# Input tiles from ScalarE's queue, and the bias tables' three copies issued apart, in a hybrid attention trunk layer

## The chip, the cores and the metric

One core of one Trainium2 chip. The metric is the device time of one execution in microseconds, the median of the runs.

## The reference

One layer of a diffusion trunk on 128 context tokens and 512 sample tokens of width 1024, all in float32. For both groups:

```
sh1, sc1, gt1, sh2, sc2, gt2 = adaln(c, w_mod, b_mod)
h = modulate(rmsnorm(x, g_mix_pre), sh1, sc1)
qa, ka, va, qb, kb, vb = project(h, w_in)
oa = neighborhood_attn(qa, ka, va, cache_a_k, cache_a_v, rpb_a)   # context tokens: full attention
ob = window_attn(qb, kb, vb, cache_b_k, cache_b_v, sink_b)
x = x + gt1 * rmsnorm(merge_heads(oa, ob, g_a, g_b, w_out), g_mix_post)
h = modulate(rmsnorm(x, g_ffn_pre), sh2, sc2)
x = x + gt2 * rmsnorm(conv_ffn(h, w_up, conv_w, conv_b, w_down), g_ffn_post)
```

The neighbourhood attention adds a bias to its scores that is gathered from `rpb_a` (8 heads, 15 x 31 entries): `bias = rpb[:, drow, dcol]`.

## The kernel before

A float32 product is made of three matmuls over high and low parts, so each weight block is loaded, rounded by ScalarE to its high part and subtracted by GpSimd or VectorE to its low part. The program is written out by hand in the order in which each engine gets its instructions; nothing reorders them later.

**The head.** `load_xt` (L200) loads five tiles of 128 tokens, xs0 to xs3 of the sample tokens in two halves each (64 rows picked by a pattern) and the context tokens as tile 4. For each tile `x_norm` takes ScalarE's square with a row sum (`junk`), GpSimd's root (`rxr`) and VectorE's scaling, and `x_trans` has PE transpose it into `xnT`. The modulation needs eight column blocks of `w_mod`, wm0 to wm7, each of two transfers of 512 KB (`load_wm`, L229); PE turns one into shift and scale by 16 small matmuls (`ada_a`, tile `psada`) and two more (`ada_c`, tile `pscol`).

**The v projection** is the loop over k = 0 to 7: `hidden(k)` makes block k of the modulated tokens, `va_mm(t, k)` adds its product for five token tiles into five PSUM banks (`psv`). The v weights come in four blocks vw0 to vw3 (`load_vw`, L236), each good for two k; `vw_split` makes the high part `vwh` on ScalarE and the low part `vwl` on GpSimd. At the end of each step k the loop issues later loads, ahead of the step's successor. The q and k projections (`psg`) follow and take 1024 x 128 blocks from a stream (`Stream`, tile `wst`): the first block wst0 is loaded at k = 2, the second at k = 4.

**The bias tables** are made in three stages through DRAM. `load_scr` (L241) has VectorE scale the 8 rows of `rpb_a` into two padded copies `rpx` and copies each of them 16 times into `scr`, in one transfer from 8 partitions. `load_ftab` (L249) copies `scr`, read with a skewed pattern, to `ftab` (1920 pieces of 128 bytes per transfer). `load_traw` reads one head's table back. Each stage waits for the one before it.

**Queues.** All loads are issued by SyncE (SP), in program order; ScalarE issues a few output transfers. A transfer tells of its landing by one of eight semaphores (DMAHW0 to DMAHW7 in the order listings), which are taken in turn over both queues, so a transfer that takes a semaphore again is issued only when its last user has landed.

Of the kernel before, what the change touches and what calls it, by code (L numbers as in the profile page):

```python
# [26 lines left out]
def trunk_kernel(  # L27
# [8 lines left out]
    nc = tc.nc  # L36
    xp = x_prompt[0]
# [36 lines left out]
    def U(shape, name, dt=F32):  # L74
        return up_.tile(shape, dt, tag="u", name=name)
# [3 lines left out]
    def WS(shape, name, i=None, dt=F32):  # L79
        if i is None:  # L80
            i = wsn[0] = 1 - wsn[0]
        return ws_.tile(shape, dt, tag=f"ws{i}", name=name)
# [13 lines left out]
    def SM(shape, name):  # L96
        return sm_.tile(shape, F32, tag="sm", name=name)
# [9 lines left out]
    def act(out, in_, func=ACTF.Copy, **kw):  # L107
        return nc.scalar.activation(out=out, in_=in_, func=func, **kw)  # L108
# [4 lines left out]
    def ts(out, a, s1, s2, op0, op1=None, eng=None):  # L113
        e = eng or nc.vector
        if op1 is None:
            return e.tensor_scalar(out=out, in0=a, scalar1=s1, scalar2=None, op0=op0)
        return e.tensor_scalar(out=out, in0=a, scalar1=s1, scalar2=s2, op0=op0, op1=op1)  # L117
# [59 lines left out]
    xt = [xp_[t // 2][:, t % 2, :] for t in range(5)]  # L177
    xsj = xs.rearrange("(r j c) d -> j r c d", r=8, j=8, c=8)
# [16 lines left out]
    def load_rows(n):  # L195
        for _ in range(n):
            src, dst = rows.pop(0)
            nc.sync.dma_start(out=dst, in_=src)

    def load_xt(t):  # L200
        if t == 4:
            nc.sync.dma_start(out=xt[4], in_=xp)
        else:
            for jj in range(2):
                nc.sync.dma_start(out=xt[t][jj * 64:jj * 64 + 64, :], in_=xsj[2 * t + jj])

# [6 lines left out]
    def rev(ap, o, n):  # L215
        return bass.AP(tensor=ap.tensor, offset=ap.offset + 14 * 31 + o, ap=[list(ap.ap[0]), [-31, 15], [1, n]])
# [7 lines left out]
    def load_late():  # L224
        nc.sync.dma_start(out=rp, in_=rpb_a[0])
        nc.sync.dma_start(
            out=sink, in_=sink_b[0].rearrange("a b -> (a b)").unsqueeze(0).to_broadcast([128, 8]))

    def load_wm(k):  # L229

        t = wm[k] = U([128, 2, KD, 128], f"wm{k}")
        for i in range(2):
            o = i * D + k * 128
            nc.sync.dma_start(out=t[:, i], in_=wmod[:, o:o + 128].rearrange("(k p) f -> p k f", p=128))

    def load_vw(st):  # L236
        w = WS([128, 2, 512], "vw")
        nc.sync.dma_start(
            out=w, in_=win[st * 256:st * 256 + 256, 1024:1536].rearrange("(k p) f -> p k f", p=128))
        vw[st] = w  # L240

    def load_scr():
        ts(rpx[0][:, :, 15:31], rev(rp, 7, 16), 8.0, None, ALU.mult)
        ts(rpx[1][:, :, 8:39], rev(rp, 0, 31), 8.0, None, ALU.mult)
        for v in range(2):
            nc.sync.dma_start(
                out=scr[v].rearrange("q (h a) w -> h q (a w)", h=8),
                in_=rpx[v].rearrange("p a w -> p (a w)").unsqueeze(1).to_broadcast([8, 16, 720]),
            )  # L249

    def load_ftab():
        for v in range(2):
            sv = scr[v, 0]
            nc.sync.dma_start(
                out=ftab[v].rearrange("q (a k) -> q a k", k=32),
                in_=bass.AP(tensor=sv.tensor, offset=sv.offset + 15, ap=[[120 * PW - 1, 16], [PW, 120], [1, 32]]),
            )
# [3 lines left out]
    def load_traw(h):  # L261
        traw[h] = t = PB([128, 2, 256], f"traw{h}")
        for v in range(2):
            for jj in range(2):
                fv = ftab[v]
                nc.sync.dma_start(
                    out=t[jj * 64:jj * 64 + 64, v, :],
                    in_=bass.AP(tensor=fv.tensor, offset=fv.offset + jj * 8 * 3840 + h * 480,
                                ap=[[32, 8], [3840, 8], [1, 256]]))

    load_xt(0)
    load_xt(1)
    load_xt(2)
    load_rows(2)
    load_xt(3)
    load_wm(0)
    load_xt(4)
    load_rows(3)
    load_vw(0)
    load_wm(1)  # L280
    load_wm(2)
    load_vw(1)
    load_wm(3)
    load_late()
    load_rows(6)
    load_wm(4)
    load_wm(5)
# [44 lines left out]
    def rows_late():  # L332
        ps = PS("o", "psr1")
        nc.tensor.transpose(ps[:, 0:32], rows1[96:128, :], ident[96:128, 96:128])
        nc.vector.tensor_copy(T1[:, 72:104], ps[:, 0:32])
        for o, n in ((W_GF, 8), (W_GMP, 16)):
            ts(T1[:, o:o + n], T1[:, o:o + n], D ** 0.5, None, ALU.mult, eng=nc.gpsimd)
        ts(nsink, sink, -1.0, None, ALU.mult, eng=nc.gpsimd)
# [63 lines left out]
    def ada_a(k, i):  # L402
        if i == 0:
            mps[k] = PS("o", "psada")
        ada_mm(mps[k], lambda j: wm[k][:, i, j, :], 128 * i, 128)
        if i == 1:
            m = PB([128, 512], "m_sb")
            act(m[:, 0:256], mps[k][:, 0:256])
            mps[k] = m

    def ada_c(k):
        ps_ = PS("s", "pscol")
        m = mps[k]
        for i in range(2):
            nc.tensor.matmul(ps_[:, 2 * i:2 * i + 2], m[:, i * 128:i * 128 + 128], sel[:, 0:2], start=True, stop=True)
        bb = lambda i: T1[:, W_MODT + 8 * i + k:W_MODT + 8 * i + k + 1].to_broadcast([128, 2])
        tt(S1[:, k, :], ps_[:, 0:2], bb(0), ALU.add)
        tmp = SM([128, 2], "gtmp")
        tt(tmp, ps_[:, 2:4], bb(1), ALU.add)
        ts(G1[:, k, :], tmp, 1.0, T1[:, W_GM + k:W_GM + k + 1], ALU.add, ALU.mult)  # L420

    def vw_split(st):
        wh = wr_.tile([128, 2, 512], F32R, tag="wh", name="vwh")
        wl = wr_.tile([128, 2, 512], F32R, tag="wl", name="vwl")
        for j in (slice(0, 1), slice(1, 2)) if st == 0 else (slice(0, 2),):
            act(wh[:, j], vw[st][:, j])
            tt(wl[:, j], vw[st][:, j], f(wh[:, j]), ALU.subtract, eng=nc.gpsimd)
        vwt[st] = (wh, wl)

    def hidden(k):  # L430
        kb, kk = k // 4, k % 4
        if k == 4:
            hH[1] = U([128, 4, T], "hH1", F32R)
            hL[1] = U([128, 4, T], "hL1", F32R)
        hf = QT([128, T], "hf")
        for c_, t_ in ((slice(512, 640), 0), (slice(0, 512), 1)):
            g_, s_ = G1[:, k, t_:t_ + 1], S1[:, k, t_:t_ + 1]
            act(hH[kb][:, kk, c_], xnT[kb][:, kk, c_], ACTF.Identity, scale=g_, bias=s_)
            ts(hf[:, c_], xnT[kb][:, kk, c_], g_, s_, ALU.mult, ALU.add)
        tt(hL[kb][:, kk, :], hf, f(hH[kb][:, kk, :]), ALU.subtract)  # L440
        for hx, hs in ((hxH, hH[kb]), (hxL, hL[kb])):
            nc.gpsimd.tensor_copy(hx[:, k, 0:64], f(hs[:, kk, 448:512]))
            nc.gpsimd.tensor_copy(hx[:, k, 64:128], f(hs[:, kk, 0:64]))

    def va_mm(t, k):
        wh, wl = vwt[k // 2]
        l_ = (hxH[:, k, :], hxL[:, k, :]) if t == 1 else (hh(k, 0, VS[t]), hh(k, 1, VS[t]))
        mm3(pv_[t], l_[0], l_[1], wh[:, k % 2, :], wl[:, k % 2, :], k == 0, k == KD - 1)
# [3 lines left out]
    def load_cc(p):  # L452
        cc = CC[p] = FP([128, 3, 128], "cc")
        nc.sync.dma_start(out=cc[:, 0], in_=ck_a[:, p * 128:p * 128 + 128])
        nc.sync.dma_start(out=cc[:, 1], in_=cv_a[:, p * 128:p * 128 + 128])
# [15 lines left out]
    for k in range(KD - 1):  # L471
        for j, t in enumerate(VO):
            va_mm(t, k)
            if j == 1:
                ada_c(k + 1)
                hidden(k + 1)
                if k == 6:
                    stream.split()
            if j == 3 and k < 6:
                ada_a(k + 2, 0)  # L480
                ada_a(k + 2, 1)
        if k % 2 == 0 and k < 6:
            vw_split(k // 2 + 1)
        if k < 2:
            load_wm(k + 6)
        if k == 2:
            load_vw(3)
            stream.load()
            rows_late()
        if k == 3:  # L490
            act(SM([128, 1], "warm"), zero, ACTF.Exp)
        if k == 4:
            load_scr()
            load_ftab()
            stream.load()
            load_cc(0)
        if k == 5:
            load_traw(0)
            load_traw(1)
# [1494 lines left out]
```

## Time and profile before

| what | value |
|---|---|
| median of 3 runs | 863.63 us (859.67 to 864.28) |
| the profiled execution, its own time | 864.4 us |
| its span, first to last instruction | 862.6 us |
| PE matmuls busy | 804.0 us, 93% of the span |
| VectorE, ScalarE, GpSimd busy | 562.8, 435.5, 295.5 us |
| mean granted TensorE clock | 0.985 |
| moved by DMA | 107.77 MB, 125 GB/s over the span |

Times in rows are microseconds from the span's start. A busy PE is counted by modelled ends of pipelined matmuls. The idle time that a timeline shows in brackets is that of the engine just before the instruction, with what ended it.

### The profile page before, as it was taken

Reading aid. Unit: us, or ns where it says so; the run is one execution under the profiler, and the core shown is the slowest. Engines: PE = TensorE matmul, PEld = TensorE weight load, DVE = VectorE, ACT = ScalarE, POOL = GpSimd, SP = SyncE. Lnnn points to the kernel's source line nnn. Section 1 sums busy time; section 2 is a strip of 40 time slices with the busy share of each in tenths; the row PEclk is TensorE's granted clock in tenths of the full one; section 3 lists DMA queues with packets and bytes.
Section 4 is the critical chain, followed back from the end, with each engine's and each line's share of the span. In section 5 each row is a group of like instructions: output and inputs, shape, how many; then the busy total and the mean of one; then the engine's idle time right before and its main releaser. Section 6 shows DMA issues by size and latency. Waiting matters only on the chain.

```text
span 862.6 us, 13868 instructions
## 1 busy us (share of the span) xinstructions
PE 804.0 (93%) x5280; PEld 702.5 (81%) x5280; DVE 562.8 (65%) x1023; ACT 435.5 (50%) x876; POOL 295.5 (34%) x353
## 2 busy tenths in 40 slices
PE   2897999999999999998989999999999999999996
PEld 2666878888778777868988999999999988888885
DVE  1543566655788885476479898898898874332115
ACT  3443567745578886457346445455455544332112
POOL 1443244424131211155954564564564200000001
PEclk9899999999999998999999999999999999999999
DMA  6996644363522122657223333332432336534313
GB/s 140 267 241 112 177 140 129 111 171 101 130 74 75 25 74 68 205 182 211 73 65 100 109 113 93 116 113 82 126 115 80 123 105 222 173 113 154 118 49 122
DMA packets 144277, 107.77 MB, mean 125 GB/s; under 512 B 16440, under 2 KB 125268, under 8 KB 144212
## 3 DMA queue, kind: packets, MB, share of 16 engines
q1 hardware_dynamic: 143204, 106.25, 42.0%
q8 instruction: 41, 0.67, 0.3%
q10 hardware_dynamic: 1008, 0.66, 0.3%
q14 instruction: 24, 0.20, 0.1%
HBM read 93.02 MB, written 14.36 MB: 124 GB/s over the span
## 4 chain that ended last, share of the span: by engine, by line
PE 46%; DVE 29%; DMA 9%; ACT 8%; issue 5%; SPq 2%; POOL 1%; DVEq 0%; POOLq 0%; ACTq 0%
PE psd L127 18%; PE psg L127 9%; DVE cv L120 7%; DVE ou L111 4%; DVE cv L111 4%; DVE owl L111 3%; PE psya L127 3%; PE zx L127 3%; PE psS L127 2%; PE psyb L127 2%; ACT cv L108 2%; DVE yy L111 2%; DMA scr<-rpx 2%; PE psO L127 2%; ACT P L108 2%
## 5 line engine op out<-in xcount | busy, mean ns | idle before, releaser
L127 PE MATMUL psd<-dwh,a 128*128 128x512 f32 x440 | 138.4, 395 | 0.0
L111 POOL TENSOR_TENSOR wsum<-wraw 128x512 f32<-128x512 f32 x36 | 70.4, 1976 | 105.3 <-DVE osb L111 50.6
L127 PEld LDWEIGHTS psd<-dwh,a 128*128 128x128 f32 x440 | 83.0, 189 | 19.9 <-ACT dwh L108 0.2
L127 PE MATMUL zx<-h2H,ou 128*128 128x322 f32 x392 | 94.9, 312 | 1.4 <-DVE yy L111 0.9
L127 PE MATMUL psd<-dwl,a 128*128 128x512 f32 x220 | 87.2, 397 | 0.8 <-DVE dwl L111 0.8
L111 DVE TENSOR_TENSOR dwl<-wd,dwh 128x1024 fp32r<-128x1024 f32 x22 | 26.9, 1225 | 89.7 <-ACT dwh L108 89.7
L127 PE MATMUL psg<-hH,wh 128*128 128x320 f32 x224 | 76.4, 341 | 7.4 <-ACT T L108 3.4
L108 ACT ACTIVATE dwh<-wd 128x1024 fp32r<-128x1024 f32 x22 | 23.3, 1059 | 94.4 <-PE psd L127 87.5
L127 PE MATMUL psg<-hH,wl 128*128 128x320 f32 x224 | 70.5, 315 | 0.0
L127 PE MATMUL psg<-hL,wh 128*128 128x320 f32 x224 | 70.5, 315 | 0.0
L127 PEld LDWEIGHTS zx<-h2H,ou 128*128 128x128 f32 x392 | 68.0, 189 | 2.0 <-DVE yy L111 1.2
L117 POOL TENSOR_SCALAR rdv<-ssdc 128x1 f32<-128x1 f32 x5 | 1.5, 300 | 179.1 <-ACT jk L108 179.1
L127 PE MATMUL zx<-h2L,ou 128*128 128x322 f32 x196 | 60.8, 310 | 0.0
L127 PEld LDWEIGHTS psg<-hH,wh 128*128 128x128 f32 x224 | 43.1, 192 | 16.7 <-ACT T L108 7.2
L108 ACT ACTIVATE cv<-yy,T 128x642 f32<-128x642 f32 x20 | 17.7, 885 | 65.7 <-DVE yy L111 65.7
L127 PEld LDWEIGHTS psd<-dwl,a 128*128 128x128 f32 x220 | 41.4, 188 | 10.8 <-DVE dwl L111 1.1
L120 DVE SCALAR_TENSOR_TENSOR cv<-yy,T,cv 128x641 f32<-128x641 f32 x40 | 35.4, 884 | 17.9 <-ACT cv L108 17.2
L127 PE MATMUL yy<-tg,oc 128*128 128x322 f32 x216 | 39.1, 318 | 5.7 <-DVE oc L111 5.7
L111 POOL TENSOR_TENSOR wl<-wst,wh 128x1024 fp32r<-128x1024 f32 (+1 forms) x12 | 27.7, 2311 | 48.3 <-ACT wh L108 31.6
L127 PEld LDWEIGHTS psg<-hL,wh 128*128 128x128 f32 x224 | 43.2, 193 | 0.5
L127 PEld LDWEIGHTS psg<-hH,wl 128*128 128x128 f32 x224 | 43.0, 192 | 0.0
L108 ACT ACTIVATE P<-P,nm 128x320 f32<-128x320 f32 (+3 forms) x64 | 40.3, 630 | 3.7 <-DVE nm L639 3.4
(352 smaller groups left out, 2215.1 us busy)
## 6 DMA issues: line engine op xcount, KB each, us to landing
wraw<-in_w_up_dram SPq DMA_DIRECT2D x40, 512.0 KB
wms<-in_w_mod_dram SPq DMA_DIRECT2D x32, 512.0 KB
wd<-in_w_down_dram SPq DMA_DIRECT2D x22, 512.0 KB
wm<-in_w_mod_dram SPq DMA_DIRECT2D x16, 512.0 KB
aD<-cv SPq DMA_DIRECT2D x22, 321.0 KB
ar<-aD SPq DMA_DIRECT2D x11, 642.0 KB
wst<-in_w_in_dram SPq DMA_DIRECT2D x10, 512.0 KB
yD<-Y SPq DMA_DIRECT2D x5, 512.0 KB
```

The lines of the kernel that those rows point to most:

```text
L108: return nc.scalar.activation(out=out, in_=in_, func=func, **kw)
L111: return (eng or nc.vector).tensor_tensor(out=out, in0=a, in1=b, op=op)
L117: return e.tensor_scalar(out=out, in0=a, scalar1=s1, scalar2=s2, op0=op0, op1=op1)
L120: return nc.vector.scalar_tensor_tensor(out=out, in0=a, scalar=s, in1=b, op0=op0, op1=op1)
L127: return nc.tensor.matmul(out, l, r, start=start, stop=stop, skip_group_check=True, **kw)
```

## The change

Four things move. `load_xt` takes a queue: tile 0 stays on SP, tiles 1 to 4 are issued by ScalarE, ahead of its first square. On SP, the first v block stands ahead of `b_mod` and its companions, and `load_late` (the bias table's source and the sinks) stands two blocks earlier. `load_scr` is called at k = 0 instead of k = 4. `load_ftab` is called at k = 3; at k = 4 the second streamed block is now the first load.

```diff
-    def load_xt(t):
+    def load_xt(t, eng):
         if t == 4:
-            nc.sync.dma_start(out=xt[4], in_=xp)
+            eng.dma_start(out=xt[4], in_=xp)
         else:
             for jj in range(2):
-                nc.sync.dma_start(out=xt[t][jj * 64:jj * 64 + 64, :], in_=xsj[2 * t + jj])
+                eng.dma_start(out=xt[t][jj * 64:jj * 64 + 64, :], in_=xsj[2 * t + jj])
...
-    load_xt(0)
-    load_xt(1)
-    load_xt(2)
+    load_xt(0, nc.sync)
+    load_xt(1, nc.scalar)
     load_rows(2)
-    load_xt(3)
+    load_xt(2, nc.scalar)
     load_wm(0)
-    load_xt(4)
+    load_xt(3, nc.scalar)
+    load_vw(0)
+    load_xt(4, nc.scalar)
     load_rows(3)
-    load_vw(0)
     load_wm(1)
+    load_late()
     load_wm(2)
     load_vw(1)
     load_wm(3)
-    load_late()
     load_rows(6)
...
         if k < 2:
             load_wm(k + 6)
+        if k == 0:
+            load_scr()
         if k == 2:
             load_vw(3)
             stream.load()
             rows_late()
         if k == 3:
             act(SM([128, 1], "warm"), zero, ACTF.Exp)
+        if k == 3:
+            load_ftab()
         if k == 4:
-            load_scr()
-            load_ftab()
             stream.load()
             load_cc(0)
```

ScalarE at the program's start, before (`junk,ssx` is the square of a tile; xs_128 holds tiles 0 and 1, xs_129 tiles 2 and 3, xs_130 tile 4):

```order
L108 ACTIVATE cpad<-cst 128x1 [waits DVE_49]
L108 ACTIVATE junk,ssx<-xs_128 128x1024 [waits DMAHW1_49,DMAHW0_49]
L108 ACTIVATE junk,ssx<-xs_128 128x1024 [waits DMAHW3_49,DMAHW2_49]
L108 ACTIVATE xnT_182<-pxs 128x4x128 [waits PE_49]
L108 ACTIVATE junk,ssx<-xs_129 128x1024 [waits DMAHW5_49,DMAHW4_49,Activation_49]
```

and now:

```order
L108 ACTIVATE cpad<-cst 128x1 [waits DVE_49]
L205 DMA xs_128<-in_x_sample_dram 64x1x1024 x2
L205 DMA xs_129<-in_x_sample_dram 64x1x1024
L205 DMA xs_129<-in_x_sample_dram 64x1x1024 [waits DMAHW0_49]
L205 DMA xs_129<-in_x_sample_dram 64x1x1024 [waits DMAHW2_49]
L205 DMA xs_129<-in_x_sample_dram 64x1x1024 [waits DMAHW4_49]
L202 DMA xs_130<-in_x_prompt_dram 128x1024 [waits DMAHW7_49]
L108 ACTIVATE junk,ssx<-xs_128 128x1024 [waits DMAHW3_49,DMAHW1_49]
```

Seven transfers now stand ahead of the first square. The four with a wait stand behind the landing of both halves of tile 1 (semaphores 0 and 2), of the first half of tile 2 (4), and of the transfer that took semaphore 7 first, SP's fifth one that has no wait, the first half of wm0.

SP in the v projection's loop, before (wm_416 is wm6, wm_470 wm7, the second `vw` vw3, the first `wst` wst0):

```order
L238 DMA vw<-in_w_in_dram 128x2x512 [waits DMAHW4_49,Pool_49]
L234 DMA wm_416<-in_w_mod_dram 128x8x128 [waits DMAHW5_49]
L234 DMA wm_416<-in_w_mod_dram 128x8x128 [waits DMAHW6_49]
L234 DMA wm_470<-in_w_mod_dram 128x8x128 [waits DMAHW7_49,PE_49]
L234 DMA wm_470<-in_w_mod_dram 128x8x128 [waits DMAHW0_49]
L238 DMA vw<-in_w_in_dram 128x2x512 [waits DMAHW1_49,Pool_49]
L350 DMA wst<-in_w_in_dram 128x8x128 [waits DMAHW4_49,DMAHW2_49,Pool_49]
L246 DMA scr<-rpx 8x16x720 [waits DMAHW3_49,DVE_49]
L246 DMA scr<-rpx 8x16x720 [waits DVE_49]
L254 DMA ftab<-scr 1920x1x32 [waits DMAHW5_49,DMAHW3_49]
L254 DMA ftab<-scr 1920x1x32 [waits DMAHW6_49,DMAHW4_49]
L350 DMA wst<-in_w_in_dram 128x8x128 [waits DMAHW7_49,DMAHW1_49,Pool_49]
```

and now:

```order
L238 DMA vw<-in_w_in_dram 128x2x512 [waits DMAHW4_49,Pool_49]
L234 DMA wm_416<-in_w_mod_dram 128x8x128 [waits DMAHW5_49]
L234 DMA wm_416<-in_w_mod_dram 128x8x128 [waits DMAHW6_49]
L246 DMA scr<-rpx 8x16x720 [waits DMAHW7_49,DVE_49]
L246 DMA scr<-rpx 8x16x720 [waits DMAHW0_49,DVE_49]
L234 DMA wm_474<-in_w_mod_dram 128x8x128 [waits DMAHW1_49,PE_49]
L234 DMA wm_474<-in_w_mod_dram 128x8x128 [waits DMAHW2_49]
L238 DMA vw<-in_w_in_dram 128x2x512 [waits DMAHW3_49,Pool_49]
L351 DMA wst<-in_w_in_dram 128x8x128 [waits DMAHW4_49,DMAHW2_49,Pool_49]
L254 DMA ftab<-scr 1920x1x32 [waits DMAHW7_49,DMAHW5_49]
L254 DMA ftab<-scr 1920x1x32 [waits DMAHW6_49,DMAHW0_49]
L351 DMA wst<-in_w_in_dram 128x8x128 [waits DMAHW3_49,Pool_49]
```

The two `scr` copies went from behind the first streamed block to a place right behind wm6 and ahead of wm7, vw3 and that block; `ftab` still stands behind it and ahead of the second block.

## Rows read from the trace of the kernel before

**Rows 1.** The page, busy time of PE (share of the span)

```profile
PE 804.0 (93%) x5280; PEld 702.5 (81%) x5280; DVE 562.8 (65%) x1023; ACT 435.5 (50%) x876; POOL 295.5 (34%) x353
```

**Rows 2.** The chain of waits, 0 to 140 us: start, length, what

```profile
3.51 9.96 DMA xs<-in_x_sample_dram
...
43.12 8.14 DMA vw<-in_w_in_dram
...
60.37 15.67 DMA scr<-rpx
76.06 0.56 SPq L254
76.72 5.95 DMA wst<-in_w_in_dram
```

**Rows 3.** Timeline of PE: start, length, what, idle before and what ended it

```profile
22.13 0.65 PE L383 MATMUL psada<-wm,cpad 128*32 128x128 f32 x16 [0.82 <-DMA wm<-in_w_mod_dram]
...
31.74 0.50 PE L127 MATMUL psv<-vwh,hH 128*128 128x512 f32 x1
...
54.91 0.51 PE L127 MATMUL psv<-vwl,hH 128*128 128x512 f32 x1 [1.23 <-POOL vwl L111]
...
65.73 0.39 PE L127 MATMUL psv<-vwl,hH 128*128 128x512 f32 x1
...
78.56 0.38 PE L127 MATMUL psg<-hH,wh 128*128 128x320 f32 x1 [1.67 <-DVE V L111]
...
83.77 0.33 PE L618 MATMUL pst<-ident,cc 128*128 128x128 f32 x1 [1.44 <-DMA cc<-in_cache_a_k_dram]
...
86.18 0.63 PE L127 MATMUL psg<-hH,wh 128*128 128x320 f32 x1 [2.09 <-DVE q L111]
```

**Rows 4.** Windows, PE: stretch, length, busy (x), granted clock, DMA share, GB/s

```profile
42.00:60.00 18.00, 16.60 (x156) 1.00 1.12 297
...
60.50:70.00 9.50, 9.50 (x73) 1.00 0.47 51
70.00:71.60 1.60, 1.60 (x8) 1.00 0.98 125
71.80:75.20 3.40, 3.40 (x21) 1.00 0.47 50
75.20:76.80 1.60, 1.60 (x12) 1.00 0.54 87
86.20:89.50 3.30, 3.30 (x12) 0.50 0.86 239
89.50:92.00 2.50, 2.50 (x18) 0.99 0.78 227
```

**Rows 5.** Timeline of SP's queue: start, length of issue, transfers

```profile
13.49 6.49 SPq L202 DMA_DIRECT2D xs<-in_x_prompt_dram  x1
...
46.02 6.86 SPq L234 DMA_DIRECT2D wm<-in_w_mod_dram  x4
52.98 1.68 SPq L238 DMA_DIRECT2D vw<-in_w_in_dram  x1
...
60.01 0.68 SPq L246 DMA_DIRECT2D scr<-rpx  x2
68.88 7.74 SPq L254 DMA_DIRECT2D ftab<-scr  x2
```

**Rows 6.** Timeline of ScalarE

```profile
7.49 1.06 ACT L108 ACTIVATE junk<-xs 128x1024 fp32r<-128x1024 f32 x1 [5.28 <-DMA xs<-in_x_sample_dram]
...
25.17 1.06 ACT L108 ACTIVATE junk<-xs 128x1024 fp32r<-128x1024 f32 x1 [2.85 <-DMA xs<-in_x_prompt_dram]
...
59.98 1.05 ACT L108 ACTIVATE vwh<-vw 128x1024 fp32r<-128x1024 f32 x1
...
72.72 4.20 ACTq L1167 DMA_DIRECT2D out_dram<-vo  x1
```

**Rows 7.** Timeline of GpSimd, the low half of vw3

```profile
61.12 2.39 POOL L111 TENSOR_TENSOR vwl<-vw,vwh 128x1024 fp32r<-128x1024 f32 x1 [0.54 <-ACT vwh L108]
```

## The prediction

> **What bounds the kernel now.** I read the page first, for the engine that fills the span: PE is busy for 93% of it [rows 1]. So time is lost or won only where PE waits, or where it runs at the lower clock. The change touches the first 95 us, and the next view is the chain of waits there. It shows what ended last: after the first input tiles, the third streamed weight block of the v projection (vw, issued at 43.12), then 15.67 us of the copy `scr<-rpx`, then the block `wst` issued only at 76.72 [rows 2]. The reader should see that the chain stands on transfers there, while PE was mostly busy beside them.
>
> The timeline of PE tells what that cost. The v projection's first matmul is at 31.74. PE idles 1.23 us at 54.91, and then 1.67, 1.44 and 2.09 us before 78.56, 83.77 and 86.18, together 5.20 us [rows 3]. After the last of these it restarts at the lower of its two clock levels: in the window from 86.2 to 89.5 the granted clock is 0.50 (1.2 GHz) and 12 matmuls take 3.3 us, while from 89.5 on 18 take 2.5 us [rows 4]. Twelve at that pace are 1.67 us, so the restart loses 1.6 us. These 6.8 us are all that the second half of the change can give back.
>
> The windows on the DMA engines come last, and they decide the case. From 42 to 60 us the engines are full (share 1.12, 297 GB/s): the weights arrive just in time. From 60.5 to 70, with only the two `scr` copies under way, the share is 0.47 at 51 GB/s: half of the engines are busy, slowly. At 68.88 SP issues the first `ftab` copy [rows 5]. The rate rises to 125 GB/s with a share of 0.98 until 71.6, falls back to 50 until 75.2, and rises again to 87 when the second `scr` copy ends [rows 4]. So the idle half of the engines did its part of `ftab` at once, and the other half did its part only after `scr`: an engine serves SP's transfers in the order of issue, and `scr` holds about eight of the sixteen.
>
> **Part by part.** *1. The `scr` copies move up, from behind all weights to a place ahead of wm7, vw3 and wst0.* They are issued at k = 0 now, and SP reaches them right after wm6. In the trace SP starts wm6 and wm7 (four transfers) at 46.02 and vw3 at 52.98 [rows 5]; VectorE's `rpx` now stands behind the second hidden block and is long done. What `scr` was behind before and is ahead of now is wm7 (2 x 0.52 MB), vw3 (0.52) and wst0 (0.52), 2.1 MB, at 297 GB/s 7.0 us. The copies began to move at about 60.4, after their issue at 60.01 [rows 5], so now at about 53.4. The second copy took 7.2 us after the first (SP's two `ftab` issues, each released by one of them, are at 68.88 and 76.06 [rows 2, 5]), so two need 14.4, and they hold half of the engines until 67.8. A weight transfer is spread over all engines and is not there until the blocked half has done its share, so wm7 and vw3 (1.57 MB, 5.3 us) land at about 73.1.
>
> Who waits: ScalarE's split of vw3 started at 59.98 without idling [rows 6], and GpSimd's half of that split ended at 61.12 + 2.39 = 63.51 [rows 7], 3.5 us after it. Now it ends at 73.1 + 3.5 = 76.6. PE's first matmul with its result ran at 65.73 [rows 3]. **Term: 76.6 - 65.7 = +10.9 us.** The bounds are the landing of vw3. If the earlier start of the weights at the head saves the pauses of the engines there, it is 2 us sooner; if `scr` moves more slowly beside the weights, as the full share of 1.12 allows, 3 us later: +8.9 to +13.9. I take 10.9, since in rows 4 `scr` kept its pace (51 and 50 GB/s) with and without waiting copies behind it. wm7 lands before vw3 and adds nothing.
>
> *2. `ftab` and the second streamed block.* In the trace both waited for `scr` to land (SP at 68.88 for 7.74 us [rows 5], `wst` at 76.72). Now `ftab` is issued once wst0 is, near 75, and the block once GpSimd has left its buffer, near 78; with the 5.95 us of rows 2 it is there at 84, and PE asks for it at 76.6 plus the 15 us of matmuls that lie between 65.73 and 86.18 (20.45 less the 5.20 idle), so at 92. The idle 1.44 and 2.09 us go. The 1.67 us come from ScalarE, held for 4.20 us in the issue of an output at 72.72 [rows 6] while `scr` and `ftab` filled the queue; that issue is now at about 84, behind both. **Term: -5.2 us.** Bounds: -5.2, and -3.5 if that hold stays.
>
> *3. Clock.* PE stands nearly idle for ten microseconds before 76.6, longer than before 86.18, so it will restart at 0.50. The 1.6 us move from one place to the other. **Term: 0**, between -1.6 (it doesn't fall) and +1.6 (it falls twice).
>
> *4. Input tiles on ScalarE's queue.* Transfers take eight completion semaphores in turn over both queues, and one that reuses a semaphore is issued when its last transfer has landed. ScalarE must issue all seven transfers before its first square, and the last (the prompt tile) waits for the first half of wm0. Before, the first square ran at 7.49, the last at 25.17, and PE started the v projection 6.6 us after that [rows 3, 6]. Now the first square runs at the earliest when xs2's first half has landed and the tile is issued (SP's wait for that half ended at 13.49 [rows 5], plus 1, so 14.5), at the latest when wm0 is there (PE's wait for it ended at 22.13 [rows 3]). Behind ScalarE's wait stand the five squares, and behind each GpSimd's root, VectorE's scaling and PE's transposes. All tiles have nearly arrived by then; with 1.06 us for a square and as much again for the copy and the hand-overs to the next one, I estimate 9 us from the first square to the last. The last is at 24 to 31, the v projection starts at 31 to 38. I take 35.5, +4, between -1 and +6. **Term: 0**, because PE would be that much later at 65.7 and then wait that much less for vw3; the cover is the 10.9 us of part 1. Without it the price is 4 less the 1.2 us idled at 54.91, since vw2 would no longer be late: +2.8.
>
> *5. vw0, the table's source rows and the rows of gains* change places by one or two transfers within the full stretch; 0, under the same cover.
>
> **Sum.** +10.9 - 5.2 + 0 + 0 = +5.7 us on the profiled execution of 864.4, so 870.1. That execution is 0.8 above the median of the runs shown, so I forecast 869.3 for the median. Over the bounds the sum runs from 8.9 - 5.2 - 1.6 = +2.1 to 13.9 - 3.5 + 1.6 = +12.0.
>
> **The rivals.** *Faster: the copies do not hold the weights.* If `scr` leaves its engines free for the weights behind it, vw3 lands by 62.2 and PE never waits: 5.2 and 1.6 us go, and the median is 856.8. For it: the copy moves only 51 GB/s, which leaves most of what the engines can carry. Against it: `ftab` stood still behind `scr` on just these engines [rows 4]. It decides at vw3: each microsecond after 62.2 costs one, and beyond 69 us nothing is left of the gain. The Trainium skill (DMA: Bandwidth & Descriptors, section Anatomy of one DMA) gives 2.0 us plus the bytes over 436 GB/s for a transfer; that would be an estimated 2.8 us for each 0.37 MB copy, vw3 at 64.4, and a median of 859.0. It is a fit for transfers of GpSimd, and the trace disagrees: 15.67 us for the two.
>
> *No change: copies harmless, head late.* Then part 4 loses its cover: -6.8 + 2.8 = -4.0, 859.6. For it stands the order in which ScalarE issues; against it the same rows as above. The Trainium skill (same page, section Issuing engines are not separate DMA queues) says that starting transfers on several engines saves only the time of the sequencer that starts them. By that the head would come out as before, 856.8 in this case. SP's prompt tile took 6.49 us to issue [rows 5], so here the sequencer's time is not small, and no run yet shows two queues loading at once.
>
> *Balance.* vw3 lands near 68 and what it costs is what the later stalls give: 863.6.
>
> *Slower still.* `scr` takes a third longer among the weights: 4.8 us more, 874.
>
> **How the numbers follow.** The forecast, with its bounds, gets 0.66; copies harmless 0.12; harmless with a late head 0.10; balance 0.05; slower still 0.07. A measurement of this kernel tells about 0.5%, 4.3 us, from no change: below 859.3 is faster, above 867.9 slower. Of the forecast's 0.66 I put 0.16 under 867.9, since its middle is only 1.4 above that. Faster is 0.12, no change 0.16 + 0.10 + 0.05 = 0.31, slower 0.50 + 0.07 = 0.57. The range 859.5 to 877 leaves out the 0.12 below and some 0.05 above. The forecast's own range, from its bounds, is 866 to 875.
>
> **What would show it.** Right: in the changed trace ScalarE's split of vw3 starts near 73 and PE idles some 10 us before the v projection's k = 6, split between wm7's side matmuls and vw3; the window after 54 us shows a DMA share near 0.5; PE has no wait between 78 and 95 but those of restart; the first square is at 14 to 22. Wrong: vw3 split before 63, or PE without a wait over 3 us there; or the first 140 us as long as before with the loss elsewhere, which would mean that work after the tables absorbed it.

## The result, and the profile after

The changed kernel takes 868.92 us (median of 13 runs, 866.2 to 873.95). The kernel before takes 863.63 in 13 runs beside it. The ratio of the two over these runs is 1.0058, with a 95% interval from 1.0036 to 1.0081: about 5 us slower. The profiled execution has a span of 866.7 us against 862.6, that is 4.1 more, with a mean granted clock of 0.983 against 0.985.

The page of the changed kernel, busy times [rows 1] and the queue that carries ScalarE's transfers (packets, MB, share of the engines; before, 1008 packets and 0.66 MB):

```profile
PE 803.4 (93%) x5280; PEld 703.0 (81%) x5280; DVE 562.2 (65%) x1023; ACT 435.8 (50%) x876; POOL 294.7 (34%) x353
...
q10 hardware_dynamic: 1584, 2.75, 1.3%
```

PE is busy for as long as before, so its busy time does not show the loss; its waits and its clock do. The chain of waits of the changed kernel, 0 to 140 us [rows 2] (start, length, what):

```profile
60.91 10.57 DMA vw<-in_w_in_dram
71.56 1.07 ACT vwh L108
72.70 2.35 POOL vwl L111
75.10 2.76 PE psv L127 x5
```

The copy `scr<-rpx`, 15.67 us long in the chain of before, has left it. In its place stands the last v block vw3, on its way for 10.57 us, and behind it one after the other ScalarE's rounding, GpSimd's low half and PE. SP's queue [rows 5] and the windows on PE [rows 4] (stretch, length, busy of PE, PEld, DVE, ACT and POOL with instructions, granted clock, DMA share, GB/s) tell why:

```profile
48.61 2.55 SPq L246 DMA_DIRECT2D scr<-rpx  x2
51.25 9.56 SPq L234 DMA_DIRECT2D wm<-in_w_mod_dram  x2
60.91 5.74 SPq L238 DMA_DIRECT2D vw<-in_w_in_dram  x1
66.74 0.42 SPq L351 DMA_DIRECT2D wst<-in_w_in_dram  x1
67.25 5.55 SPq L254 DMA_DIRECT2D ftab<-scr  x2
75.07 0.39 SPq L351 DMA_DIRECT2D wst<-in_w_in_dram  x1
```

```profile
42.00:53.00 11.00, 11.00 (x106) 8.35 (x105) 5.09 (x13) 4.57 (x8) 5.46 (x11) 1.00 1.10 301
53.00:60.00 7.00, 7.00 (x63) 5.62 (x62) 3.09 (x9) 3.39 (x6) 4.77 (x8) 1.00 0.71 132
60.00:66.00 6.00, 6.00 (x57) 4.61 (x55) 2.89 (x9) 1.59 (x3) 1.43 (x4) 1.00 0.62 94
66.00:70.00 4.00, 0.97 (x18) 0.41 (x16) 0.19 (x1) 0.00 (x0) 0.00 (x0) 1.00 0.87 252
70.00:73.00 3.00, 2.66 (x19) 1.43 (x19) 0.00 (x0) 1.44 (x3) 0.30 (x1) 0.51 1.05 252
73.00:76.00 3.00, 1.70 (x3) 0.80 (x4) 1.99 (x1) 0.97 (x2) 3.00 (x4) 0.50 0.77 107
76.00:80.00 4.00, 4.00 (x12) 3.32 (x13) 1.26 (x5) 0.94 (x2) 0.36 (x3) 0.50 0.75 215
...
75.10:81.30 6.20, 6.20 (x18) 4.86 (x19) 2.76 (x8) 2.15 (x3) 2.24 (x6) 0.58 0.57 161
```

The engines are full to 53 us. Then the rate falls to 132 and 94 GB/s, just while SP holds wm7 (9.56 us in issue) and vw3 (5.74 us) behind the two copies; at 66 the copies are through and the rate is 252 again. PE of the changed kernel [rows 3] pays at the place that was forecast:

```profile
35.11 0.50 PE L127 MATMUL psv<-vwh,hH 128*128 128x512 f32 x1
...
37.23 0.50 PE L127 MATMUL psv<-vwh,hL 128*128 128x512 f32 x1 [1.39 <-DVE hL L111]
...
68.51 0.65 PE L384 MATMUL psada<-wm,cpad 128*32 128x128 f32 x16 [2.18 <-DMA wm<-in_w_mod_dram]
...
70.13 1.08 PE L384 MATMUL psada<-wm,cpad 128*32 128x128 f32 x16 [0.98 <-DMA wm<-in_w_mod_dram]
...
73.05 0.80 PE L127 MATMUL psv<-vwh,hH 128*128 128x512 f32 x1 [0.26 <-ACT hH L108]
...
75.10 0.80 PE L127 MATMUL psv<-vwl,hH 128*128 128x512 f32 x1 [1.25 <-POOL vwl L111]
```

The first matmul with the low half of vw3 runs at 75.10, against 65.73 before: 9.4 us later. The idle times in brackets make 4.7 us of it. PE was 2.6 us late already, and the rest, some 2 us, goes with the lower clock level: after the idle times of 2.18 and 0.98 us the granted clock is 0.51 from 70 to 73 us and 0.50 (1.2 GHz) from there to 80. The matmul at 75.10 takes 0.80 us, the same one 0.39 before [rows 3]. The last of the waits is the one for vw3's low half, so it alone sets the 75.10; the late head and the slow matmuls ahead of it lie under it. ScalarE [rows 6] and GpSimd [rows 7] of the changed kernel:

```profile
2.54 14.52 ACTq L205 DMA_DIRECT2D xs<-in_x_sample_dram  x5
...
20.16 1.06 ACT L108 ACTIVATE junk<-xs 128x1024 fp32r<-128x1024 f32 x1 [17.94 <-DMA sel<-in_sel_c_dram]
...
71.56 1.06 ACT L108 ACTIVATE vwh<-vw 128x1024 fp32r<-128x1024 f32 x1 [8.91 <-DMA vw<-in_w_in_dram]
...
84.43 0.35 ACTq L1170 DMA_DIRECT2D out_dram<-vo  x1
```

```profile
72.70 2.35 POOL L111 TENSOR_TENSOR vwl<-vw,vwh 128x1024 fp32r<-128x1024 f32 x1 [9.77 <-ACT vwh L108]
```

ScalarE spends the first 20 us on its own DMA issues; the first square comes 12.7 us later than before. Its later issue of `vo` takes 0.35 us where it took 4.20. PE has no listed wait between 77 and 100 us any more, where before it had three, of 2.1, 1.7 and 1.4 us [rows 3].

Where the time went, worked out from the start of the same matmul in both traces: PE is 4.5 us late at 35 to 51 us (time of before), 2.6 at 56 to 60, 11.7 at 68 to 76, and 4.3 at 90 us. It is 5.4 to 6.0 between 111 and 200 us, 4.5 again at 260, and 4.1 at the end. So the difference at the end is as large as the one made in the first 90 us, of a loss of 11.7 and a gain of 7.4.

### The profile page after: what moved, and what is told of

It reads as the page before. It is cut to its first block, busy times and chain, and to the rows that moved or that the text cites. A ratio compares the mean times of both kernels' runs of the same rounds, so it can differ in the third digit from the quotient of the medians.

```text
span 866.7 us, 13874 instructions
## 1 busy us (share of the span) xinstructions
PE 803.4 (93%) x5280; PEld 703.0 (81%) x5280; DVE 562.2 (65%) x1023; ACT 435.8 (50%) x876; POOL 294.7 (34%) x353
## 4 chain that ended last, share of the span: by engine, by line
PE 47%; DVE 29%; ACT 8%; DMA 6%; issue 5%; POOL 1%; SPq 1%; DVEq 0%; POOLq 0%; ACTq 0%
PE psd L127 18%; PE psg L127 8%; DVE cv L120 7%; DVE ou L111 4%; DVE cv L111 4%; DVE owl L111 3%; PE psya L127 3%; PE psv L127 3%; PE zx L127 3%; PE psS L127 2%; PE psyb L127 2%; ACT cv L108 2%; DVE yy L111 2%; DMA out_dram<-ko 2%; ACT P L108 2%
## 5 line engine op out<-in xcount | busy, mean ns | idle before, releaser
L127 PEld LDWEIGHTS psg<-hH,wh 128*128 128x128 f32 x224 | 42.6, 190 | 12.7 <-ACT T L108 7.3
```

The source lines that it names most:

```text
L127: return nc.tensor.matmul(out, l, r, start=start, stop=stop, skip_group_check=True, **kw)
```

## Experiments

Two theories went in. **Hold:** the two `scr` copies hold half of the DMA engines ahead of wm7 and vw3, and the late head hides under the wait that this makes. **Head:** the late start on ScalarE's queue is what costs, and the copies are harmless. Each ratio below is to the kernel before, run beside it (medians 864.76, 864.68 and 865.54 us in the three groups of runs).

**1. The tables alone.** The kernel before, with only the three stages put apart; all tiles on SP.

```diff
+        if k == 0:
+            load_scr()
...
+        if k == 3:
+            load_ftab()
         if k == 4:
-            load_scr()
-            load_ftab()
             stream.load()
```

> The kernel before with only the table stages moved (scr at k = 0, ftab at k = 3, the second streamed block first at k = 4); all input tiles on SyncE's queue in the old order. Theory: the head is as before, and PE still waits for vw3 until about 75 to 77; the two parts of the change overlap, so this alone costs nearly as much as both: +4 to +6 us, 868 to 869.5. Rival (head): the late stalls go and nothing is paid, -6.8, 857.

Measured: 869.24 us, ratio 1.0044 [1.0015, 1.0072]. The timeline of PE in that run (the wait for wm7 and for vw3):

```profile
66.74 1.08 PE L383 MATMUL psada<-wm,cpad 128*32 128x128 f32 x16 [4.98 <-DMA wm<-in_w_mod_dram]
...
73.37 0.79 PE L127 MATMUL psv<-vwl,hH 128*128 128x512 f32 x1 [1.25 <-POOL vwl L111]
```

This is inside the theory's range. With a head that was even 2 us early, vw3's low half is still used 7.6 us later than before, and PE is 2.7 us late at 90 us. The hold needs no late head.

**2. The head alone.** The changed kernel with the table stages back at k = 4.

```diff
-        if k == 0:
-            load_scr()
...
-        if k == 3:
-            load_ftab()
         if k == 4:
+            load_scr()
+            load_ftab()
             stream.load()
```

> The changed kernel with both table stages put back to k = 4, so that only the loads at the head differ from the kernel before. Theory (the loss is the time for which the two scr copies hold half of the DMA engines ahead of wm7 and vw3): vw3 is in time, so the late head shows: the v projection starts some 4.4 us later than 31.74, the 1.2 us before vw3's predecessor go, the three idle times before the k projection stay: about +3 us, 866 to 867. Rival (the loss is the seven transfers that ScalarE issues ahead of its first square): the whole loss is here, +5 us, 868 to 869.

Measured: 870.72 us, ratio 1.0056 [1.0029, 1.0082]. This is a miss for the theory's price and above the rival's too. The first square is at 18.31 and the v projection starts 1.5 us late; PE is 2.6 us late to 51 us, 0.7 late at 56 to 76, and 0.6 late at 90 to 106. Of the three late stalls two are there, longer than before, 5.3 us together (waits of PE, 77 to 100 us):

```profile
PE psg L127 <- DVE q L111: 2.8, 1, 2.8
PE pst L619 <- DMA cc<-in_cache_a_k_dram: 2.5, 1, 2.5
```

The third, the wait for V, is gone, and with it the long issue of `vo` on ScalarE, although the copies stand as late as before:

```profile
73.41 0.35 ACTq L1168 DMA_DIRECT2D out_dram<-vo  x1
```

The rest of that execution's 4.0 us comes far behind the head: PE is 2.3 us late at 112 and 4.9 late at 415, where the granted clock is 0.88 to 0.89 from 105 to 120 and 0.89 from 395 to 405, and was 1.00 in the trace of before. So this run alone gives no clean price of the head; run 7 is made for that.

**3 to 5. Copies from 128 partitions.** `rp` is loaded 16 times over, so that `rpx` stands on 128 partitions, and each `scr` copy is one row block per partition: the same bytes to `scr`, the same place in SP's order. (The load of the source rows, `rp`, grows from 15 to 238 KB.) Applied to the changed kernel, to the tables alone, and to the kernel before.

```diff
-    rp = FP([8, 15, 31], "rp")
+    rp = FP([128, 15, 31], "rp")
...
-    rpx_ = PT([8, 2, 15, PW], "rpx")
+    rpx_ = PT([128, 2, 15, PW], "rpx")
...
-        nc.sync.dma_start(out=rp, in_=rpb_a[0])
+        r0 = rpb_a[0]
+        nc.sync.dma_start(out=rp, in_=bass.AP(tensor=r0.tensor, offset=r0.offset, ap=[[0, 16], [465, 8], [1, 465]]))
...
-                out=scr[v].rearrange("q (h a) w -> h q (a w)", h=8),
-                in_=rpx[v].rearrange("p a w -> p (a w)").unsqueeze(1).to_broadcast([8, 16, 720]),
+                out=scr[v].rearrange("q (h a) w -> (q h) (a w)", h=8),
+                in_=rpx[v].rearrange("p a w -> p (a w)"),
```

> The changed kernel with the 8 table rows loaded 16 times into 128 partitions, so that each scr copy leaves from 128 partitions and runs on all 16 DMA engines; same bytes, same place in SyncE's order. Theory: a copy takes 1 to 2 us instead of 7 to 8, vw3 lands near 60 to 63, PE waits for neither wm7 nor vw3 (under 2 us), and only the late head is left against the late stalls saved: 859 to 861. Rival (head): as the changed kernel, 868 to 869.

> The kernel before with the table stages moved as in the change and the scr copies made from 128 partitions; input tiles on SyncE's queue. Theory: neither the head nor vw3 is late, and the idle 5.2 us and the restart's 1.6 us before the k projection go: 856 to 858, the fastest of the four. Rival (something else in moving the tables costs time, a buffer or the ftab stage at k = 3): over 861.

> The kernel before with one edit: rp and rpx on 128 partitions, so that scr is written from all of them; every transfer stays in its place, scr behind wst0. Theory (the late stalls of the kernel before come from the length of the narrow copies): the second streamed block and the cache tile arrive in time, the 5.2 us of idle time at 78 to 86 us and perhaps the 1.6 us of restart go, 857 to 861, about the same as the wide copy with the stages moved up (858.9): moving them is worth nothing by itself. Rival (the stages had to be moved up): 863 to 865, the stalls stay.

Measured: the change with wide copies 861.81 us, 0.9952 [0.9917, 0.9987]; the tables alone with wide copies 858.91, 0.9916 [0.9886, 0.9945]; the kernel before with wide copies and nothing moved 859.13, 0.9923 [0.9893, 0.9953]. The third lies in its theory's range; the first two lie 0.8 and 0.9 us above theirs, and all lie below their rivals' times. In the first, SP, ScalarE and the windows (compare 132 and 94 GB/s above):

```profile
48.18 3.75 SPq L247 DMA_DIRECT2D scr<-rpx  x2
52.02 2.23 SPq L235 DMA_DIRECT2D wm<-in_w_mod_dram  x2
54.34 2.40 SPq L239 DMA_DIRECT2D vw<-in_w_in_dram  x1
```

```profile
61.94 1.05 ACT L108 ACTIVATE vwh<-vw 128x1024 fp32r<-128x1024 f32 x1
```

```profile
53.00:56.00 3.00, 3.00 (x44) 2.26 (x43) 2.50 (x5) 0.60 (x2) 3.00 (x4) 1.00 1.02 346
56.00:60.00 4.00, 3.73 (x18) 2.80 (x19) 1.86 (x7) 2.73 (x5) 1.71 (x5) 1.00 1.12 315
```

wm7 is issued in 2.23 us instead of 9.56, and vw3 is split 9.6 us sooner, without a wait. With the place of the copies kept and only their shape changed, the loss turns into a gain: at 90 us PE is 5.5 us ahead of the kernel before, where the change is 4.3 behind it. The shape is what cost. In the third, SP's rows show how short the two copies now are, since `ftab` waits for them:

```profile
61.67 0.85 SPq L247 DMA_DIRECT2D scr<-rpx  x2
65.05 1.83 SPq L255 DMA_DIRECT2D ftab<-scr  x2
```

The first `ftab` copy is released 3.4 us after the first `scr` issue, and both are issued after 5.2; in rows 5 the two stand 8.9 and 16.1 us [rows 2, 5] behind it. PE's only listed waits from 50 to 100 us are 1.2 for vw2's low half and 0.6 for `hL`: the late stalls are gone where nothing was moved. Hence the rival of this run, that the stages had to move, falls: 0.9923 without the move, 0.9916 with it.

The number of engines does not account for all of the narrow copy's slowness: two wide copies, 0.74 MB, are through in 5.2 us, so at 142 GB/s or more, nearly three times the 51 of rows 4, with at most twice the engines. The wide copy also reads 128 partitions instead of 8, and no run separates the number of partitions read from the number of engines. What makes the narrow copy slow on the engines that it holds stays open.

**6. One copy early.** The change, with the second copy back behind wst0 (`load_scr1(v)` issues one copy).

```diff
+        load_scr1(0)
...
         if k == 3:
+            load_scr1(1)
             load_ftab()
```

> The change with one of the two narrow scr copies early (at k = 0) and the other back behind wst0, ahead of ftab. Theory (what vw3 loses is the time for which the copies ahead of it hold half of the engines): with one copy of about 7 us ahead, vw3 lands some 7 us earlier than with two, near 64.5, its split is done near 68 where PE, 2.5 us late from the head, asks for it: no wait over 2 us for wm7 or vw3, late stalls mostly gone, 860 to 864. Rival (the early place itself delays the weights, whatever the size of what stands there, by the order of the completion semaphores): vw3 lands near 70 again, 867 to 870.

Measured: 861.33 us, ratio 0.9969 [0.9939, 0.9999]. Timeline of ScalarE:

```profile
64.27 1.06 ACT L108 ACTIVATE vwh<-vw 128x1024 fp32r<-128x1024 f32 x1 [0.84 <-DMA vw<-in_w_in_dram]
```

vw3 comes at 64.3 with one copy ahead of it and 71.5 with two: 7.3 us for a copy, which is the 7.2 us between the two `ftab` releases of before. The time is inside the theory's range, and at 90 us PE is 3.3 us ahead of the kernel before. The hold scales with the bytes ahead; together with run 3, where the copies have the early place and PE waits for no weight, that leaves no sign of a cost of the place itself.

**7. The head without the tables' cover.** The head alone with wide copies, to be read against the kernel before with wide copies.

```diff
-    load_xt(0)
-    load_xt(1)
-    load_xt(2)
+    load_xt(0, nc.sync)
+    load_xt(1, nc.scalar)
...
```

> Head changed as in the change (tiles 1 to 4 on ScalarE), stages of the tables in their old places, scr copied from 128 partitions: against the kernel with the wide copy and nothing else (859.1, its vw3 split at 62.5 without a wait of PE over 1.3 us) only the head differs. Theory (an uncovered late head costs what it comes later, less the 1.2 us that PE would wait at 55): first square at 18 to 20, PE 2.5 to 3.5 us later from 31 us on, 1 to 2.5 us later than the wide copy alone at 90, 861 to 863. Rival (the head costs the 5 us that the run of the head alone showed): 863.5 to 865. Second rival (it costs nothing where the copies are wide): 858 to 860.

Measured: 861.55 us, ratio 0.9956 [0.9928, 0.9983], against 0.9923 without the head: 0.33%, 2.9 us. The first square is at 19.98 and PE 4.7 us late from 35 to 51; at 90 us PE is 1.3 us behind the run without the head. All of this is as the theory said. With the tables moved as well the ratios differ as much (0.9952 against 0.9916, 3.1 us). But the intervals overlap in both pairs, and the traces do not bear out 3 us: with the tables moved (runs 3 and 4) the head is 2.9 us late at 35 to 51 us, and at 90 us PE is 0.3 us ahead of the run without it. So the head costs some 3 us in the medians, 1.3 and -0.3 in the first 90 us of the traces, and where the rest arises is not shown.

**8. Only tile 1 on ScalarE.** The head alone, with tiles 2 to 4 back on SP.

```diff
-    load_xt(2, nc.scalar)
+    load_xt(2, nc.sync)
...
-    load_xt(3, nc.scalar)
+    load_xt(3, nc.sync)
...
-    load_xt(4, nc.scalar)
+    load_xt(4, nc.sync)
```

> The head alone, with only tile 1 left on ScalarE's queue (two transfers, neither with a wait) and tiles 2 to 4 back on SP; the stages of the tables as before. Theory (the head is late because ScalarE's issues of tiles 2 to 4 wait for landings, and its squares stand behind them): the first square is back at 7 to 9 us, the v projection starts at 31 to 32.5, 863 to 866. Rival (the head is late by the new order of SP's own transfers, or by two queues loading at once): the v projection stays 2 us or more late, 868 to 871 as with the head alone.

Measured: 868.17 us, ratio 1.0048 [1.0018, 1.0079]. The head did what the theory said (the v projection starts at 31.88), the time did not: it lies in the rival's range. Timeline of ScalarE, and windows on PE:

```profile
8.29 1.06 ACT L108 ACTIVATE junk<-xs 128x1024 fp32r<-128x1024 f32 x1 [6.08 <-DMA xs<-in_x_sample_dram]
```

```profile
110.00:140.00 30.00, 28.91 (x236) 24.62 (x225) 18.63 (x66) 19.58 (x56) 13.76 (x38) 0.94 0.46 131
140.00:200.00 60.00, 59.00 (x485) 51.13 (x484) 33.18 (x118) 34.81 (x98) 19.94 (x39) 0.97 0.47 128
200.00:260.00 60.00, 55.09 (x452) 47.91 (x451) 44.52 (x142) 37.15 (x102) 18.45 (x31) 0.95 0.42 109
```

PE is on time from 35 to 51 us and 0.3 us early at 90. It is then 1.5 us late at 115, 3.8 at 170, 5.4 at 260 and 7.0 at the end; the clock is granted at 0.66 from 110 to 115 us, and at 0.94, 0.97 and 0.95 in the windows above. Before, the same windows read:

```profile
110.00:140.00 30.00, 29.28 (x237) 24.79 (x238) 19.08 (x67) 20.32 (x58) 13.79 (x37) 1.00 0.46 131
140.00:200.00 60.00, 59.38 (x511) 51.34 (x510) 35.56 (x124) 35.80 (x99) 21.68 (x39) 1.00 0.46 130
200.00:260.00 60.00, 55.05 (x444) 46.94 (x443) 45.09 (x146) 37.16 (x104) 17.89 (x34) 0.97 0.41 108
```

So PE falls behind after the edited part, in stretches with less clock, and not at the head. Over all timed runs its mean granted clock is 0.981, that of before 0.986 (averages of the clocks listed with the runs). A straight line through all timed runs, with a level for each kernel, gives 2.3 us for 0.005 of clock, so by this estimate about half of the 4.2 us of the ratio goes with the clock. Why the clock is granted less often there was not found.

The eight kernels together, ratio to before, and in brackets how late PE is at 90 us in the one traced execution of each (us, minus is early):

| | copies from 8 partitions | from 128 partitions |
|---|---|---|
| as before | 1 (0) | 0.9923 (-5.1) |
| tables moved | 1.0044 (2.7) | 0.9916 (-5.2) |
| tiles on ScalarE | 1.0056 (0.6) | 0.9956 (-3.7) |
| both (the change) | 1.0058 (4.3) | 0.9952 (-5.5) |

The best are the two without the ScalarE head and with wide copies. They are faster than the kernel before and the change, and no difference between them can be measured; the simpler one moves nothing. Most of what the wide copies give is there at 90 us; of the 4.8 us that the 1.0056 of the tiles alone stands for, only 0.6 is.

## Why the prediction was right, point by point

*Part 1, the hold: right, 1.5 us too large.* The term was +10.9; measured is +9.4 (75.10 against 65.73). The landing of vw3 was put at 73.1 and was 71.5, inside the bounds. Two of its signs came only in part: PE was to idle some 10 us there and idles 4.7, the rest of the 9.4 being the late head and the lower clock; and the DMA share was to be near 0.5 and is 0.71 and 0.62. Runs 3 and 6 show the mechanism: take the hold away by shape or by half and the loss goes. The Trainium skill (DMA: Bandwidth & Descriptors, Rules for kernel authors) says that a transfer whose outermost dimension is under 16 is confined to at most that many engines. The trace agrees for the copy with 8 in front, which shows a share of 0.47 with nothing beside it [rows 4].

*Part 2, the late stalls: right in size, one cause not borne out.* The 1.67, 1.44 and 2.09 us are gone, and the hold on ScalarE's issue of `vo` with them (0.35 for 4.20 us): -5.2. The prediction put the 1.67 us to `scr` and `ftab` filling the queue. In run 2 `scr` and `ftab` are issued as late as before and `vo` is issued between the two `ftab` copies as before; its issue takes 0.35 us, and the wait for V is gone there too. So what held that issue is not shown.

*Part 3, the clock: within its bounds.* The term was 0 with ±1.6. The granted clock is at its lower level from 70 to 80 us. What that costs before 75.10 lies under the wait for vw3. From 75.10 to 81.30 the mean is 0.58, so 0.42 of 6.2, that is 2.6 us, are lost, and the 1.6 us at 86 are not lost any more: +1.0.

*Part 4, the head: right in time, covered for the most part, its price uncovered not settled.* First square 20.16 (14.5 to 22 was said), v projection at 35.11 (35.5). PE's 4.5 us are down to 2.6 at 56 us, since vw2 is no longer waited for. Against the tables alone the change is 4.6 us late at 56 us and 1.6 at 90: two thirds vanish in the wait for wm7 and vw3. The ratios, 1.0044 and 1.0058, are too close to tell. Uncovered the head was priced at +2.8; the medians of runs 5 and 7 give 2.9, those of 3 and 4 3.1, and their traces 1.3 and -0.3 at 90 us.

*Part 5.* The table's source rows move ahead of five transfers (wm2, vw1 and wm3), and not of one or two. No run separates this; nothing in the trace shows a wait for them.

*Sum.* +9.4 - 5.2 + 1.0 = +5.2 against a forecast of +5.7. In the traces PE is 4.3 us late at 90 us: the stalls and the restart gave back 7.4 us where the terms have 6.8, and 0.3 came back ahead of them. The profiled span grew by 4.1, the ratio of 1.0058 is 5.0 us of 863.6. So the mechanism was right, and that the number came out so close (869.3 against 868.92) is partly luck: the hold was 1.5 us too large and the clock 1.0 too small, and the medians differ by 1 us more than the traces do.

*The rivals.* Copies harmless and harmless with a late head (856.8 and 859.6) fall with run 1 and with the wait for vw3 in the changed trace. They describe what wide copies do where the tables are moved: 858.9 without the head (run 4) and 861.8 with it (run 3), each 2 us above. Balance and slower still would have needed vw3 at 68 or 4.8 us of further delay; it was 71.5.

## What to carry to other kernels

When a transfer moves ahead in a queue, ask how many DMA engines it occupies and what now stands behind it: here one copy from 8 partitions made the weights behind it 7.3 us late, and the same bytes from 128 partitions cost nothing that PE waited for. Change the shape of such a copy before its place; here the shape alone gave all of the gain. A load put on the queue of an engine that also computes delays that engine's first work by every wait in front of its issues: here the first square went from 7.49 to 20.16 us, and to 8.29 where only the two loads without a wait stood there. How much of that reaches the end depends on whether something later makes PE wait anyway. And one trace beside the medians tells where a loss is made: here two kernels 0.5% slower had lost nearly nothing at 90 us of their traces.

## What was not expected

The clock carries part of the difference between these kernels far from the edits. In run 8 the first 90 us are as fast as before, and 7.3 us are lost later, some of it at places where the granted clock is lower. By the lists of the timed runs the mean granted clock is 0.980 for the tables alone, 0.981 for run 8, 0.984 for the change, 0.985 for the head alone, 0.985 to 0.986 for the kernel before, and 0.988 to 0.989 for the four kernels with wide copies and the one with one copy early. Within one kernel it ranges widely too: the tables alone with wide copies had a span of 853.1 us at 0.995 in one run and 862.0 at 0.980 in another. So a few us of each ratio above may be clock and not waits. With the line of run 8 taken off, the change is 3.3 us above the kernel before, the tables alone 1.7, run 8 1.2 and the head alone 4.8, each give or take 1.3 (an estimate, in which a low clock that comes of the waits themselves is taken off too). That the change itself costs by waits does not hang on this, since its 4.1 us are all there at 90 us. How the clock's share comes about stays open, and so does what makes the head alone 4.8 us slower, of which its trace has 0.6 at 90 us.
